# A weight remainder accumulated from DRAM, and the small start loads on two other queues, in a two-layer flow backbone

## The chip, the cores and the metric

One core of one Trainium2 chip. The metric is the device time of one execution in microseconds (us). The kernel before takes 2303.33 us, the median of three runs (2302.43, 2303.33 and 2305.74 us).

## What is computed

Two layers of a backbone on 128 context tokens and 512 latent tokens, 1024 channels, all in float32. Each layer modulates the normalised tokens, sends them through one wide input projection (11264 columns), runs four branches on its pieces (convolution, Hyena with an FFT, pooling, attention), gates and merges them, and projects the result back:

```python
def parallel_mixer(h, p, latent, k_ctx, v_ctx):
    u = h @ p['w_in']                                   # 1024 x 11264
    (a_glu, a_gate, b_proj, b_gate, c_in, c_gate, q, k, v, d_gate, g_merge) = jnp.split(u, points, axis=-1)
    ya = conformer_conv(a_glu, ...)                     # GLU, depthwise conv 31, layer norm, swish, pointwise
    ya = (ya * jax.nn.silu(a_gate)) @ p['wo_conv']
    filt = hyena_filters(L, ...)                        # a small MLP on positions gives the filters
    yb = (hyena(b_proj, ..., filt, ...) * jax.nn.silu(b_gate)) @ p['wo_hyena']
    yc = (multiscale_pool(c_in, p['pool_w'], ...) * jax.nn.silu(c_gate)) @ p['wo_pool']
    att = block_attention(rope(rms_norm(q)), rope(rms_norm(k)), v)
    yd = (att * jax.nn.silu(d_gate)) @ p['wo_attn']
    gm = jax.nn.sigmoid(g_merge).reshape(B, L, 4, D_MODEL)
    return (gm[:, :, 0] * ya + gm[:, :, 1] * yb + gm[:, :, 2] * yc + gm[:, :, 3] * yd) @ p['w_out'], k, v

def trunk_layer(x, cond, p, ...):
    shift, scale, gate = jnp.split(jax.nn.silu(cond) @ p['w_ada'] + p['b_ada'], 3, axis=-1)
    h = rms_norm(x, p['norm_g']) * (1.0 + scale) + shift
    y, k, v = parallel_mixer(h, p, ...)
    return x + gate * y, k, v
```

## The kernel before, in words

**Products.** TensorE multiplies in a float32 form of reduced precision. To keep float32 accuracy every factor is split in two, `hi` (the value rounded to that form) and `lo` (what is left), and each product is three matmuls: hi x hi, hi x lo, lo x hi. For a weight these are the tiles `whi` and `wlo`.

**The ring of weights.** `weights` (L331) brings in one weight tile of 128 partitions and at most 1024 columns: eight blocks of 128 rows by 128 columns for `w_in` and `wo_attn`, four blocks of 128x128 for `wo_hyena` and `wo_pool`, four blocks of 128x256 for queries, keys, values and `w_out`, one of 128x128 for `pool_w`. SyncE loads it to `raw` (two buffers, NRAW), ScalarE casts it to `whi` (three buffers, NHI), and `wlo` (three buffers) is made in one of two ways. While `pooled[0]` is set (from the first Hyena inputs on, and off again for the gates of the convolution and for the output projection), ScalarE writes -whi into `wlo` and a DMA that GpSimd issues adds `raw` to it, in SBUF (L344 and L345). Otherwise VectorE subtracts (L347). The ring holds three tiles: the next load is issued when a raw buffer is free, and a raw buffer is free when all that read it have ended, the cast and the accumulating DMA among them.

```python
            sp.dma_start(out=rv.rearrange("p (k c) -> p k c", k=kk), in_=src)
            act.copy(hi[:, 0:w], rv)
            if pooled[0]:
                act.activation(out=lo[:, 0:w], in_=r32(hi[:, 0:w]), func=AF.Copy, scale=-1.0)
                nc.gpsimd.dma_start(out=r32(lo[:, 0:w]), in_=rv, accum_op=ALU.add)
```

178 tiles take the first way. The weights are loaded in the order in which TensorE uses them; in the code such tiles have a priority ahead of the work around them (WAHEAD).

**Who sets the order.** `Loom` (L85) is a planner that runs while the program is written: work is cut into threads, and it lets the thread write its next piece whose operands are ready first by its own model of TensorE, of the element engines and of the DMA. TensorE's order is exactly the one so written; the other engines' is set by a scheduler of its own. So a load's arrival time, as `load` (L324) models it, can move matmuls, and tile numbers such as raw_121 differ between two programs without meaning anything.

**The start.** The loads of the start are written by hand, in the order of the string DORD (L32): `0` to `7` are chunks of the conditioning weight `w_ada` (two loads each, `load_chunk`, L1935; the first chunks borrow the tiles of the weight ring, raw, wlo and whi), `f`, `g`, `h`, `i` what the Hyena filters read (`fetch`, L856: decay, hy_w3, hy_b3), `x` the tokens (`load_x`, L676), `t` the FFT tables, and `s` the small loads: seven for the hidden layers of the filters (`load_hidden`, L549: zfeat, w1, b1, freq, b2 and two blocks of w2), `sel`, ten rows of parameters (`load_params`, L516) and `edge`. `load_small` (L1929) writes a few of them after each larger load (SMALL is 3 per half chunk). All of them are issued by SyncE. Ahead of them come `c_ctx`, `c` and the identity. The thread `cond` (L531) turns the conditioning rows with ScalarE's tanh, and the products with `w_ada` wait for it.

**The layer.** The first 72 us hold the start: filters, modulation, the first products with `w_ada`. Then come, for each layer, the Hyena inputs with the filters beside them, queries, keys and values, attention beside the FFT convolution, the merges of the four branches with the convolution and the pooling between them, and the output projection. GpSimd sums squares of the filters, works in the pooling, and issues the accumulating DMAs.

Of the kernel before, what the change touches and what calls it, by code (L numbers as in the profile page):

```python
# [10 lines left out]
F32R = mybir.dt.float32r  # L11
I32 = mybir.dt.int32
AF = mybir.ActivationFunctionType
ALU = mybir.AluOpType
# [14 lines left out]
NSLOT = 13  # L29
NRAW = 2  # L30
NHI = 3
DORD = "0sf4xt15gh2637"  # L32
SMALL = 3
PT = 6.5
PN = 4.0
HW = 80
# [30 lines left out]
def r32(ap):  # L67
    return ap.bitcast(F32)
# [165 lines left out]
def hybrid_flow_backbone(ctx: ExitStack, tc: tile.TileContext, i, o):  # L234
    nc = tc.nc
    lm = Loom()
# [4 lines left out]
    sp = nc.sync  # L241
# [18 lines left out]
    def nm(p):  # L260
        count[0] += 1
        return f"{p}{count[0]}"
# [58 lines left out]
            dve.scalar_tensor_tensor(out=lo, in0=src, scalar=scale, in1=r32(hi),  # L321
                                     op0=ALU.mult, op1=ALU.subtract)

    def load(dst, src):  # L324

        sp.dma_start(out=dst, in_=src)  # L326
        lm.issue = max(lm.issue, lm.pe - 2.0) + 0.48
        lm.dma = max(lm.dma, lm.issue + 1.2) + int(np.prod(dst.shape)) * 4 / 360e3
        return lm.dma + 1.9

    def weights(src, kk, n):  # L331
        yield from wr.get()
        lm.bg = True
        with tc.high_priority(offset=WAHEAD):
            raw = wp.tile([P, 1024], F32, tag="raw", name=nm("raw"), bufs=NRAW)
            hi = wp.tile([P, 1024], F32R, tag="whi", name=nm("whi"), bufs=NHI)
            lo = wp.tile([P, 1024], F32R, tag="wlo", name=nm("wlo"), bufs=NHI)
            w = kk * n
            rv = raw[:, 0:w]
            sp.dma_start(out=rv.rearrange("p (k c) -> p k c", k=kk), in_=src)  # L340
            act.copy(hi[:, 0:w], rv)
            if pooled[0]:

                act.activation(out=lo[:, 0:w], in_=r32(hi[:, 0:w]), func=AF.Copy, scale=-1.0)  # L344
                nc.gpsimd.dma_start(out=r32(lo[:, 0:w]), in_=rv, accum_op=ALU.add)  # L345
            else:
                dve.tensor_tensor(out=lo[:, 0:w], in0=rv, in1=r32(hi[:, 0:w]), op=ALU.subtract)  # L347
        lm.bg = False
        return (hi[:, 0:w].rearrange("p (k c) -> p k c", k=kk),
                lo[:, 0:w].rearrange("p (k c) -> p k c", k=kk))  # L350

    def w_cols(l, c0):
        return weights(i["w_in"][l][:, c0:c0 + 128].rearrange("(k p) c -> p k c", p=P), 8, 128)
# [58 lines left out]
    def token_proj(src, a, fn):  # L412


        bank = {}
        for kh in range(2):
            whi, wlo = yield from weights(src[512 * kh:512 * kh + 512].rearrange("(k p) c -> p k c", p=P), 4, 256)
            for t in (1, 2, 3, 4, 0):
                b = (t + 1) // 2
                first = kh == 0 and t in (0, 1, 3)  # L420
                if first:
                    bank[b] = yield from mm.get()
                else:
                    yield
                out = bank[b][:, 0:256] if t in (0, 1, 3) else bank[b][:, 256:512]
                cols = slice(128 * t, 128 * t + 128)
                for k in range(4):
                    ah, al = a.h(4 * kh + k)[:, cols], a.l(4 * kh + k)[:, cols]
                    last = kh == 1 and k == 3
                    for n, (x, y) in enumerate(((ah, whi), (al, whi), (ah, wlo))):  # L430
                        pe.matmul(out, x, y[:, k, :], start=(first and k == 0 and n == 0),
                                  stop=(last and n == 2), skip_group_check=True)
                if t == 0:
                    wr.put(WD)
                if kh == 1 and t in (0, 2, 4):
                    if t:
                        yield from fn(t - 2, bank[b].rearrange("p (t c) -> p t c", t=2))
                    else:
                        yield from fn(-1, bank[b][:, 0:256].unsqueeze(1))
                    mm.put()  # L440
# [75 lines left out]
    def load_params(s):  # L516
        rows = s.v(0, 512)
        b = 0
        r = []
        for src in (i["conv_dw_w"].rearrange("l k c -> (l k) c"), i["conv_dw_b"], i["conv_ln_g"], i["conv_ln_b"],  # L520
                    i["hy_short_w"].rearrange("l k (j c) -> (l k j) c", j=3),
                    i["hy_short_b"].rearrange("l (j c) -> (l j) c", j=3),
                    i["hy_skip"].rearrange("l k c -> (l k) c"), i["pool_scale"],
                    i["norm_g"].rearrange("l (j c) -> (l j) c", j=2),
                    i["b_ada"].rearrange("l (j c) -> l j c", c=512)[:, 0:4]):
            n = int(np.prod(src.shape[:-1]))
            r.append((rows[b:b + n, :], src, t_prm))
            b += n
        return r
# [19 lines left out]
    def load_hidden(s):  # L549

        w1, w2, cols = s.v(T, P), s.v(T + P, P), s.v(T + 2 * P, 3)
        r = [(s.v(0, T)[0:33, :], i["c_zfeat"]),
             (w1[0:33, :].rearrange("z (l h) -> z l h", l=2), i["hy_w1"].rearrange("l z h -> z l h"))]
        for c, n in enumerate(("hy_b1", "hy_freq", "hy_b2")):
            r.append((cols[:, c:c + 1], i[n].rearrange("l (h a) -> (l h) a", a=1)))
        dve.memset(w2, 0.0)
        for l in range(DEPTH):
            h = slice(64 * l, 64 * l + 64)
            r.append((w2[h, h], i["hy_w2"][l]))
        return [x + (t_hid,) for x in r]  # L560
# [35 lines left out]
    def w_ada(l, j):  # L596
        return i["w_ada"][l][:, 256 * j:256 * j + 256].rearrange("(k p) c -> p k c", p=P)
# [78 lines left out]
    def load_x(xs, prompt, sample):  # L676
        for h in range(2):
            v = xs[h].v(0, 5, 512)
            load(v[:, 0, :], prompt[:, 512 * h:512 * h + 512])
            t = load(v[:, 1:5, :], sample[:, 512 * h:512 * h + 512].rearrange("(j p) d -> p j d", p=P))  # L680
        return t
# [153 lines left out]
    class Hyena:  # L835
# [12 lines left out]
        def tables(self, s):  # L848
            self.tabE = s
            t = load(s.v(0, 2560), i["c_tab"])  # L850
            self.tf = s.v(0, 4, 2, 128)
            self.ti = s.v(1024, 4, 2, 128)
            self.tpr = s.v(2048, 4, 128)
            self.ev_tab.t = t
# [1068 lines left out]
    small = load_hidden(s_hid) + [(sel, i["c_sel"], t_prm)] + load_params(s_prm) + [(edge, i["c_edge"], t_prm)]  # L1923
# [2 lines left out]
    h0 = hys[0]  # L1926
    xs0 = [Slot(), Slot()]

    def load_small(n):  # L1929

        for dst, src, t in small[:n]:
            t[0] = load(dst, src)
        del small[:n]

    def load_chunk(j):  # L1935

        if spare:
            s, halves = None, []
            for _ in range(2):
                tag = spare.pop()  # L1940
                t = wp.tile([P, 1024], F32, tag=tag, name=nm(tag), bufs=NRAW if tag == "raw" else NHI)
                halves.append(t.rearrange("p (k c) -> p k c", k=4))
        else:
            s = Slot()
            v = s.v(0, 8, 256)
            halves = [v[:, 0:4], v[:, 4:8]]
        for kh in range(2):
            t = load(halves[kh], w_ada(0, j)[:, 4 * kh:4 * kh + 4])
            load_small(SMALL)
        chunks.append((j, s, halves, t))  # L1950

    for x in DORD:
        if x == "x":
            x_first = (xs0, sm.tile([P, 5, 2], F32, tag="ssq0", name=nm("ssq")),
                       load_x(xs0, i["x_prompt"][0], i["x_sample"][0]))
            load_small(2 * SMALL)
        elif x in "fghi":
            c, q = divmod("fghi".index(x), 2)
            if c not in h0.flt:
                h0.flt[c] = Slot()  # L1960
            h0.fetch(c, q)
        elif x == "t":
            h0.tables(Slot())
            load_small(2 * SMALL)
        elif x == "s":
            load_small(7)
        else:
            load_chunk(int(x))
    load_small(len(small))
    t_hid, t_prm = t_hid[0], t_prm[0]  # L1970
    lm.spawn(cond(s_cond, t_cond), 0)
    lm.spawn(hidden(s_hid, t_hid), 1)
# [102 lines left out]
```

## Time and profile before

| | |
|---|---|
| median of three runs | 2303.33 us |
| the profiled execution, its own time | 2302.68 us |
| its span | 2300.9 us |
| TensorE, matmuls (PE) | 2201.6 us busy, 96% |
| TensorE, weight loads (PEld, beside PE) | 2154.2 us, 94% |
| VectorE (DVE) | 1416.2 us, 62% |
| ScalarE (ACT) | 1104.7 us, 48% |
| GpSimd (POOL) | 348.8 us, 15% |

Times on the page are microseconds of one profiled execution. Issuing a DMA is not counted as busy. PEclk is the clock that was granted to TensorE, in tenths of full speed (2.4 GHz; the lower level is 1.2 GHz). The span cut into 40 slices has 57.5 us in each. The page's DMA rows tell two queues apart: q1 holds the loads and stores that SyncE issues, q0 those that GpSimd issues. A row `A <- B` of the waits says that engine A stood idle until B had ended.

### The profile page before, as it was taken

How to read it: one execution, taken by the hardware profiler on the slowest of the kernel's cores; microseconds unless marked ns; L12 is line 12 of the kernel's file. 1: busy time of each engine (PE TensorE's matmuls, PEld its weight loads, DVE VectorE, ACT ScalarE, POOL GpSimd, SP SyncE). 2: the span in 40 equal slices, each digit the busy share in tenths (PEclk: the TensorE clock that was granted, in tenths of full speed). 3: DMA queues.
4: the chain of work that ended last, by engine and by line, in shares of the span. 5: the costliest groups of instructions: out<-in, count | busy, mean ns of one | idle time of the engine just before them, and what ended most of it. 6: DMA issues, size and time to landing. Idle time of an engine off the chain costs nothing.

```text
span 2300.9 us, 39784 instructions
## 1 busy us (share of the span) xinstructions
PE 2201.6 (96%) x15951; PEld 2154.2 (94%) x15951; DVE 1416.2 (62%) x2853; ACT 1104.7 (48%) x2078; POOL 348.8 (15%) x348
## 2 busy tenths in 40 slices
PE   5998999999999999999989999999999999999999
PEld 3998999999999998999979999999999999899999
DVE  5785786556669854334466668756656897533433
ACT  4644456666664334223355453667667433422321
POOL 1633211000001111000045242000000111100000
PEclk8999999999999999999999999999999999999999
DMA  8465564444446655233545434444344576432332
GB/s 273 117 153 135 132 167 105 104 101 99 116 115 150 150 123 120 76 95 87 168 129 120 115 87 118 105 109 102 81 102 100 141 151 153 105 100 78 97 105 79
DMA packets 310440, 274.08 MB, mean 119 GB/s; under 512 B 11293, under 2 KB 279773, under 8 KB 309998
## 3 DMA queue, kind: packets, MB, share of 16 engines
q1 hardware_dynamic: 284622, 186.59, 26.9%
q0 software_dynamic: 25632, 84.95, 20.2%
q8 instruction: 125, 2.05, 0.4%
q14 instruction: 61, 0.50, 0.1%
HBM read 174.34 MB, written 12.22 MB: 81 GB/s over the span
## 4 chain that ended last, share of the span: by engine, by line
PE 75%; DVE 12%; DMA 5%; ACT 3%; issue 3%; POOL 1%; SPq 1%; POOLq 0%; ACTq 0%; DVEq 0%
PE mm L194 60%; DVE sl L179 6%; PE ax L194 6%; PE sc L194 5%; PE ax L203 4%; DVE wx L179 2%; DMA wlo<-raw 2%; DMA raw<-in_w_in_dram 1%; DVE k L179 1%; ACT u L179 1%; POOL sl L179 1%; SPq L326 1%; DVE u L179 1%; ACT wlo L179 1%; DMA sl<-in_hy_w_dram 1%
## 5 line engine op out<-in xcount | busy, mean ns | idle before, releaser
L194 PE MATMUL mm<-sl,whi 128*128 128x320 f32 x6304 | 1427.2, 314 | 7.7 <-DVE t L179 5.5
L194 PEld LDWEIGHTS mm<-sl,whi 128*128 128x128 f32 x6304 | 1058.1, 190 | 15.1 <-DVE t L179 4.8
L194 PE MATMUL mm<-sl,wlo 128*128 128x320 f32 x3152 | 982.8, 312 | 6.8 <-DMA wlo<-raw 5.9
L194 PEld LDWEIGHTS mm<-sl,wlo 128*128 128x128 f32 x3152 | 597.5, 190 | 7.6 <-DMA wlo<-raw 6.4
L179 ACT CAST whi<-raw 128x1024 fp32r<-128x1024 f32 (+2 forms) x272 | 255.4, 939 | 581.8 <-PE mm L194 419.8
L345 POOL DMA_DIRECT2D wlo<-raw x178 | 154.6, 868 | 1140.9 <-ACT wlo L179 844.3
L194 PE MATMUL mm<-whi,sl 128*128 128x256 f32 x1600 | 289.8, 283 | 0.0
L194 PEld LDWEIGHTS mm<-whi,sl 128*128 128x128 f32 x1600 | 244.9, 188 | 1.6 <-issue 0.8
L179 DVE TENSOR_TENSOR wlo<-raw,whi 128x1024 fp32r<-128x1024 f32 x94 | 95.6, 1017 | 225.1 <-ACT whi L179 224.8
L194 PE MATMUL mm<-wlo,sl 128*128 128x256 f32 x800 | 224.1, 280 | 0.8 <-DMA wlo<-raw 0.8
L194 PE MATMUL sc<-sl,sl 128*128 128x128 f32 (+1 forms) x1344 | 208.4, 298 | 10.2 <-DVE sl L179 3.9
L179 DVE SCALAR_TENSOR_TENSOR sc<-sl,prm,sc 128x640 f32<-128x640 f32 (+14 forms) x232 | 207.2, 893 | 11.2 <-ACT sc L179 6.7
L179 DVE TENSOR_TENSOR h<-ax,h 128x512 fp32r<-128x512 f32 (+1 forms) x200 | 120.6, 604 | 131.3 <-ACT h L179 130.2
L194 PEld LDWEIGHTS sc<-sl,sl 128*128 128x128 f32 x1344 | 182.4, 197 | 13.6 <-DVE u L179 5.2
L179 ACT ACTIVATE wlo<-whi 128x1024 fp32r<-128x1024 f32 (+2 forms) x178 | 174.6, 981 | 1.6
L179 DVE SCALAR_TENSOR_TENSOR t<-t,mm 128x320 f32<-128x320 f32 x192 | 93.1, 485 | 133.2 <-PE mm L194 101.5
L179 ACT ACTIVATE t<-mm 128x320 f32<-128x320 f32 x208 | 89.9, 432 | 130.8 <-PE mm L194 130.5
L194 PEld LDWEIGHTS mm<-wlo,sl 128*128 128x128 f32 x800 | 150.8, 189 | 1.0 <-DMA wlo<-raw 1.0
L179 ACT CAST h<-ax 128x512 fp32r<-128x512 f32 (+1 forms) x200 | 102.5, 514 | 70.4 <-PE ax L203 68.3
L179 DVE TENSOR_SCALAR_CACHE_REDUCE u<-sc,rq 128x640 f32<-128x640 f32 x128 | 112.7, 880 | 38.0 <-PE sc L194 36.7
L194 PE MATMUL ax<-h,sl 128*128 128x256 f32 (+1 forms) x656 | 121.8, 298 | 4.8 <-DVE h L179 4.5
L179 ACT ACTIVATE u<-u,nb 128x640 f32<-128x640 f32 x128 | 106.2, 829 | 37.8 <-DVE u L179 37.0
(194 smaller groups left out, 2208.8 us busy)
## 6 DMA issues: line engine op xcount, KB each, us to landing
raw<-in_w_in_dram SPq DMA_DIRECT2D x176, 512.0 KB
wlo<-raw POOLq DMA_DIRECT2D x152, 512.0 KB, 4.7
wlo<-in_w_ada_dram SPq DMA_DIRECT2D x19, 512.0 KB
whi<-in_w_ada_dram SPq DMA_DIRECT2D x19, 512.0 KB
raw<-in_wo_attn_dram SPq DMA_DIRECT2D x16, 512.0 KB
raw<-in_w_out_dram SPq DMA_DIRECT2D x16, 512.0 KB
sl<-in_c_decay_dram SPq DMA_DIRECT2D x16, 320.0 KB
mscr<-t SPq DMA_DIRECT2D x16, 320.0 KB
```

The source lines that it names most:

```text
L179: r = f(*args, **kw)
L194: r = self.real.matmul(out, lhsT, rhs, **kw)
L203: r = self.real.transpose(out, in_, ident)
L326: sp.dma_start(out=dst, in_=src)
L345: nc.gpsimd.dma_start(out=r32(lo[:, 0:w]), in_=rv, accum_op=ALU.add)
```

## The change

Two edits. The accumulating DMA reads the weight from its place in DRAM again and no more from `raw`; it has the shape of the raw load, so a tile of eight blocks is 1024 runs of 512 bytes, and so is its target written. `raw` is then read by the cast (or by VectorE's subtraction) alone. And the nineteen small loads of the start are written ahead of everything in DORD: the first seven are issued by ScalarE, the other twelve by GpSimd, with an arrival in the planner of 12 us or later. SyncE issues the larger loads, in the same order as before.

```diff
-DORD = "0sf4xt15gh2637"
-SMALL = 3
+DORD = "0f4xt15gh2637"
...
-    def load(dst, src):
-        sp.dma_start(out=dst, in_=src)
+    def load(dst, src, eng=None):
+        (eng or sp).dma_start(out=dst, in_=src)
+        if eng:
+            lm.dma = max(lm.dma, lm.pe + 1.2) + int(np.prod(dst.shape)) * 4 / 360e3
+            return max(lm.dma + 1.9, 12.0)
         lm.issue = max(lm.issue, lm.pe - 2.0) + 0.48
...
                 act.activation(out=lo[:, 0:w], in_=r32(hi[:, 0:w]), func=AF.Copy, scale=-1.0)
-                nc.gpsimd.dma_start(out=r32(lo[:, 0:w]), in_=rv, accum_op=ALU.add)
+                nc.gpsimd.dma_start(out=lo[:, 0:w].rearrange("p (k c) -> p k c", k=kk), in_=src.bitcast(F32R),
+                                    accum_op=ALU.add)
...
-    def load_small(n):
-        for dst, src, t in small[:n]:
-            t[0] = load(dst, src)
-        del small[:n]
+    for n, (dst, src, t) in enumerate(small):
+        t[0] = load(dst, src, nc.scalar if n < 7 else nc.gpsimd)
...
             t = load(halves[kh], w_ada(0, j)[:, 4 * kh:4 * kh + 4])
-            load_small(SMALL)
```

The other calls of `load_small` go too. What moves on the engines, at three places:

SyncE's queue at the start, before, from its fourth load on (sl_116 is what the hidden layers read, sl_117 the parameters, sl_138 the filters' decay and weights):

```order
L326 DMA raw_121<-in_w_ada_dram 128x4x256
L326 DMA sl_116<-in_c_zfeat_dram 33x640
L326 DMA sl_116<-in_hy_w_dram 33x2x64
L326 DMA sl_116<-in_hy_b_dram 128x1
L326 DMA raw_122<-in_w_ada_dram 128x4x256
L326 DMA sl_116<-in_hy_freq_dram 128x1
L326 DMA sl_116<-in_hy_b_dram 128x1
L326 DMA sl_116<-in_hy_w_dram 64x64 x2
L326 DMA sel<-in_c_sel_dram 128x2
L326 DMA sl_117<-in_conv_dw_w_dram 62x512
L326 DMA sl_117<-in_conv_dw_b_dram 2x512
L326 DMA sl_117<-in_conv_ln_g_dram 2x512
```

The same place in the change (sl_144 holds the decay now, sl_119 and sl_120 the tokens x):

```order
L325 DMA raw_140<-in_w_ada_dram 128x4x256
L325 DMA raw_141<-in_w_ada_dram 128x4x256
L325 DMA sl_144<-in_c_decay_dram 128x5x128
L325 DMA sl_144<-in_hy_w_dram 64x2x128
L325 DMA sl_144<-in_hy_b_dram 2x2x128
L325 DMA wlo_148<-in_w_ada_dram 128x4x256
L325 DMA whi_149<-in_w_ada_dram 128x4x256
L325 DMA sl_119<-in_x_prompt_dram 128x512
L325 DMA sl_119<-in_x_sample_dram 128x4x512
L325 DMA sl_120<-in_x_prompt_dram 128x512
L325 DMA sl_120<-in_x_sample_dram 128x4x512
```

The fourth half chunk of `w_ada` and the first load of x come right behind the filters' loads; the nineteen small ones are gone from this queue.

ScalarE at the start, in the change (hd is a scratch tile, sl_112 holds the conditioning rows; before, the table load stood first):

```order
L325 DMA sl_116<-in_c_zfeat_dram 33x640
L325 DMA sl_116<-in_hy_w_dram 33x2x64
L325 DMA sl_116<-in_hy_b_dram 128x1
L325 DMA sl_116<-in_hy_freq_dram 128x1
L325 DMA sl_116<-in_hy_b_dram 128x1
L325 DMA sl_116<-in_hy_w_dram 64x64 x2
L178 ACT_TABLE_LOAD
L178 ACTIVATE hd_190<-ones 2x640
L178 ACTIVATE sl_112<-sl_112 2x1024
```

Seven loads (the last row is two) stand ahead of the table load and of the tanh on the conditioning rows.

GpSimd among the filter sums of the first layer, before (k, sl and wx are tiles of the filters, frs a scale, fv sums):

```order
L345 DMA wlo_1223<-raw_1221 128x1024
L179 TENSOR_TENSOR frs_1154<-fv_1153,nhalf 128x2
L179 TENSOR_TENSOR sl_538<-sl_450,sl_138 128x640
L345 DMA wlo_1329<-raw_1327 128x1024
L179 TENSOR_TENSOR wx_189<-sl_450 128x128 x2
L179 TENSOR_TENSOR k_1165<-k_1165,k_1179 128x512
```

The same place in the change:

```order
L347 DMA wlo_1315<-in_w_in_dram 128x8x128
L178 TENSOR_TENSOR frs_1213<-fv_1212,nhalf 128x2
L178 TENSOR_TENSOR sl_508<-sl_437,sl_144 128x640
L178 TENSOR_TENSOR wx_189<-sl_437 128x128 x2
L347 DMA wlo_1423<-in_w_in_dram 128x8x128
L178 TENSOR_TENSOR k_1236<-k_1236,k_1391 128x512
```

The accumulating DMAs stand at much the same places among the sums; each now reads eight runs for each of 128 partitions where it read one.

## Rows read from the trace of the kernel before

**Rows 1.** the page: busy times, and the span in 40 slices
```profile
PE 2201.6 (96%) x15951; PEld 2154.2 (94%) x15951; DVE 1416.2 (62%) x2853; ACT 1104.7 (48%) x2078; POOL 348.8 (15%) x348
...
PEclk8999999999999999999999999999999999999999
```

**Rows 2.** windows: us, busy PE, PEld, DVE, ACT, POOL, clock, DMA, GB/s
```profile
0.00:50.00 50.00, 25.24 (x158) 11.98 (x162) 24.17 (x73) 20.63 (x47) 6.12 (x10) 0.80 0.84 269
850.00:900.00 50.00, 42.39 (x257) 41.09 (x256) 30.73 (x65) 23.52 (x41) 6.96 (x8) 0.90 0.50 113
```

**Rows 3.** waits of PE from 72 us on: total us, times, longest
```profile
PE ax L203 <- DVE sl L179: 15.2, 6, 5.8
PE mm L194 <- DMA wlo<-raw: 6.7, 3, 3.3
PE mm L194 <- DVE t L179: 5.5, 6, 2.6
```

**Rows 4.** waits of SP's queue, the whole span
```profile
SPq L340 <- DMA wlo<-raw: 1351.8, 176, 21.5
...
SPq L326 <- DMA sl<-in_conv_dw_w_dram: 1.6, 1, 1.6
```

**Rows 5.** timeline of SP, 0 to 60 us: start us, us, what
```profile
1.84 0.43 SPq L326 DMA_DIRECT2D raw<-in_w_ada_dram  x1
...
5.16 1.45 SPq L326 DMA_DIRECT2D sl<-in_hy_w_dram  x2
...
18.08 0.43 SPq L326 DMA_DIRECT2D sl<-in_x_sample_dram  x1
```

**Rows 6.** windows of the start, columns as in rows 2
```profile
5.00:20.00 15.00, 6.43 (x33) 3.36 (x34) 5.76 (x8) 2.57 (x4) 0.00 (x0) 1.00 0.65 180
20.00:40.00 20.00, 9.50 (x60) 3.62 (x60) 12.20 (x40) 10.71 (x30) 0.00 (x0) 0.67 0.99 341
40.00:50.00 10.00, 9.30 (x68) 5.00 (x71) 5.47 (x19) 3.55 (x10) 5.92 (x6) 0.64 1.04 334
```

**Rows 7.** chain of waits, 0 to 75 us: start us, us, what
```profile
44.02 8.58 DMA sl<-in_w_ada_dram
```

**Rows 8.** the tile wlo, whole span: ns min/median/max, first and last start
```profile
L345 POOL DMA_DIRECT2D wlo<-raw x178: 850/869/1024, 93.0 to 2019.6; - x178
```

**Rows 9.** timeline of ACT, POOL and PE around 740 us
```profile
730.54 1.05 ACT L179 CAST whi<-raw 128x1024 fp32r<-128x1024 f32 x1 [2.90 <-PE mm L194]
...
737.61 1.05 ACT L179 CAST whi<-raw 128x1024 fp32r<-128x1024 f32 x1 [2.90 <-PE mm L194]
...
740.23 0.87 POOL L345 DMA_DIRECT2D wlo<-raw  x1 [6.20 <-ACT wlo L179]
...
744.62 0.46 PE L194 MATMUL mm<-sl,whi 128*128 128x320 f32 x2
```

**Rows 10.** DMA issues, whole span: KB each, median us to landing
```profile
wlo<-raw POOLq DMA_DIRECT2D x152, 512.0 KB, 4.7
```

**Rows 11.** timeline of ACT, POOL and PE around 890 us
```profile
887.96 1.05 ACT L179 CAST whi<-raw 128x1024 fp32r<-128x1024 f32 x1 [2.34 <-DMA raw<-in_w_in_dram]
...
890.89 0.87 POOL L345 DMA_DIRECT2D wlo<-raw  x1 [6.86 <-ACT wlo L179]
...
896.87 0.48 PE L194 MATMUL mm<-sl,wlo 128*128 128x320 f32 x1 [2.58 <-DMA wlo<-raw]
```

**Rows 12.** DMA queues from 750 to 800 us: packets, MB, share
```profile
q0 software_dynamic: 1052, 3.85, 40.7%
q1 hardware_dynamic: 7280, 3.67, 24.9%
```

**Rows 13.** DMA queues from 872.9 to 876.4 us, with one accumulation of 64 KB
```profile
q0 software_dynamic: 144, 0.07, 15.5%
```

**Rows 14.** windows from 75 to 125 us, columns as in rows 2
```profile
75.00:100.00 25.00, 25.00 (x193) 24.23 (x192) 17.65 (x45) 14.40 (x31) 18.02 (x17) 1.00 0.37 99
```

**Rows 15.** DMA issues, 1860 to 1960 us, columns as in rows 10
```profile
wlo<-raw POOLq DMA_DIRECT2D x15, 512.0 KB, 5.5
```

More of the change, by code (lines that the diff above doesn't have):

```diff
@@ L1955, in hybrid_flow_backbone @@
                        load_x(xs0, i["x_prompt"][0], i["x_sample"][0]))
-            load_small(2 * SMALL)
         elif x in "fghi":
@@ L1963, in hybrid_flow_backbone @@
             h0.tables(Slot())
-            load_small(2 * SMALL)
-        elif x == "s":
-            load_small(7)
         else:
             load_chunk(int(x))
-    load_small(len(small))
     t_hid, t_prm = t_hid[0], t_prm[0]
```

## Prediction

> **What bounds the kernel now.** I read the page first: TensorE is busy 2201.6 of 2300.9 us, at a clock that is full in all but a few slices [rows 1]. The two parts of the change touch none of its matmuls, only their order, so all that can be won or lost is its idle time (99 us in all) and the half-clock stretches behind some of it. I then read the waits: what does TensorE wait for, and where? Some 25 us of the idle time lies in the first 50 us, while the first loads come in (PE busy 25.24 of 50 us); single stretches later lose up to 8 us, the one from 850 us 7.6 with the clock down to 0.90 [rows 2]. After 72 us the waits that end on a wlo tile come to 6.7 us, in three places; most others end on VectorE, in the filters and the convolutions [rows 3]. Against that, SyncE sits 1351.8 us before the next raw load until a wlo DMA has landed [rows 4]. That is no loss by itself, since the ring has three whi/wlo tiles; the reader should see that the long wait is SyncE's and the short one TensorE's.
>
> **Part 1, the start.** SyncE issues in order, and 19 of its first 33 DMAs are small. They take it about as long as the large ones, 0.4 us each, or more (1.45 us for the two of hy_w); it reaches the last load of x only at 18.08 us [rows 5]. Meanwhile the DMA engines are not full: a share of 0.65 from 5 to 20 us, then 0.99 and more [rows 6]. The idle part is 15 x 0.35 = 5.2 us. From 20 us on the transfers are the bound until the last w_ada chunk lands at 52.6 us, for which TensorE waits [rows 7]. The bytes stay the same, so the end of the transfers can come forward by what was idle: at most 5.2 us. Two things take some of it back. ScalarE now issues seven loads first, at 0.4 us each by SyncE's rows some 3 us, and the order shows its table load and the conditioning tanh behind them; the first w_ada product waits for that tanh, but the last chunk, which sets the end, doesn't. And SyncE's loads wait for older ones that used the same semaphore (1.6 us on conv_dw_w once [rows 4]), so it can now trip over ScalarE's loads in the first microseconds, where its raw w_ada load stood at 1.84 us before [rows 5]. I take 4 us of 5.2, with 0 and 8 as ends: 8 if x, which SyncE reaches 11 us of issuing earlier, helps the VectorE chain behind it as well. GpSimd's twelve loads are covered: its queue is empty until after 40 us (0 busy from 5 to 40 us, 5.92 us from 40 to 50) [rows 6], and twelve issues of 0.87 us [rows 8] are done by 13 us. Without that cover each would delay the first filters by 0.87 us.
>
> **Part 2, what it removes.** The accumulating DMA no longer reads raw, so a raw tile is free when its cast to whi ends, not when the wlo DMA lands. In the regular stretches that is about 7 us earlier: cast from 737.61, negation, DMA issued at 740.23 [rows 9], landing 4.7 us after the issue by the median [rows 10]. Where it costs now: at 887.96 ScalarE's cast had waited 2.34 us for raw, the wlo DMA went out at 890.89 and TensorE stood 2.58 us until 896.87 [rows 11]; the 3.3 us wait of rows 3 is the same place in the second layer. I count 5 of the 6.7 us as gone, and 1 us of clock behind them.
>
> **What it adds.** All 178 DMAs now read rows of the weight in DRAM. A projection tile of 128x1024 is then 1024 runs of 512 bytes instead of 128 of 4 KB (the raw load of the same bytes shows it: 7280 packets for seven tiles, 1040 each with 16 for the semaphore); tiles of 4x256 are runs of 1 KB. Three prices.
> (a) The packets. Accumulating 4 KB takes 0.407 x 16 x 50 us / 940 = 346 ns [rows 12]. The 64 KB tiles of pool_w are already 512-byte runs: 0.155 x 16 x 3.5 us / 128 = 68 ns [rows 13], so 4 KB would be 542 ns. A tile goes from 2.8 to 4.3 us of all 16 engines, +1.6 us. Those reads are from SBUF; from DRAM it is not shown. Plain loads in the same window take 0.249 x 16 x 50 us / 7280 = 27 ns a packet, so the source as such is not slow.
> (b) The issue. GpSimd takes 850 to 1024 ns, whatever the bytes, but always for 128 runs [rows 8]. For 1024 runs nothing here shows it. Ends: nothing more, or eight times, 6.95 us. I take 1.7 us, +0.8: nearest is the row on its own engine, in which 64 KB and 512 KB cost the same, so a fixed part dominates; an estimate. Behind it on GpSimd stand the filter sums; it is 72% busy from 75 to 100 us [rows 14], where five such DMAs cost perhaps 1 us of TensorE.
> (c) Collisions get rarer: raw loads start at a landing now, so they run into the next accumulation (5.5 us to land in the densest stretch against the median of 4.7 [rows 10, 15]). Starting at the cast they are 2.5 us ahead of it. I take -0.7 us.
> So a tile lands some 1.7 us later. What covers that is the time between landing and first use. In the regular stretch a tile of TensorE work is 7.07 us (cast to cast, 730.54 to 737.61) and the next two tiles are in hand: the one cast at 730.54 is used at 744.62 and landed at 740.23 - 7.07 + 4.7 = 737.9, so 7 us are in hand [rows 9]. I made the same reading for all 178, from the first, issued at 93.0, to the last, at 2019.6 [rows 8]: the median is 7.4 us, but 12 have under 1.7, 20 under 3, 29 under 4, 58 under 6. The shortfalls add up to 12 us at 1.7 later, 34 at 3, 57 at 4, 145 at 6, 214 at 7. About half of the 12 were late through their raw, which goes: I count 6. If a stall goes, next late is VectorE's t [rows 3].
>
> The Trainium skill speaks on (b): its page "DMA: Bandwidth & Descriptors", section "Anatomy of one DMA — SWDGE (gpsimd) path", calls descriptor generation small and says many descriptors can be emitted before they cost. By it (b) would be nothing and the sum some 3 us lower; no row here has more than 128 runs to agree or not.
>
> **Sum.** Start -4, waits for wlo -5, clock -1, later landings +6, filters +1, and -3 for what stands behind SyncE's shorter wait, stores and filter loads (an estimate with ends of -8 and +5, since the planner also writes another order on TensorE): -6 us. The profiled execution took 2302.68 us, 0.65 below the median of 2303.33, so I forecast 2297.5.
>
> **Rivals.**
> *The issue grows with the runs* (slower). GpSimd spends 3 to 7 us on each of the 152 large tiles. It decides from about 2.7 us, where the shortfalls reach what was won. At 4 us landings are 4 later: 2303 - 12 + 29 to 57, some 2330; at 6.95, 7 later, up to 214 of shortfall and the filter chain with it, 2420 to 2500. For it: the time is GpSimd's own, and it has eight times as many runs to name. Against: no dependence on anything in rows 8, with ends 0.17 us apart.
> *The DMA engines become the bound* (slower). In the dense stretch 40.7% becomes 64%, with 24.9% of loads 89% [rows 12]: still cover. If a packet from DRAM took 90 ns, 5.8 + 1.8 us would pass the 7.07 us of a tile: 0.5 us on each of some 35 tiles a layer, about +30, 2320. The same page, section "Why small descriptors are slow (HBM only)", says small runs cost on the DRAM side and not between SBUF tiles; rows 12 and 13 contradict the second half (68 ns against 346/8 = 43), so I don't lean on the first.
> *Nothing arrives* (no change). The start is hidden, because VectorE's and ScalarE's chain from 52.6 to 72 us isn't shortened, and the later landings eat what the raw tiles give: 2303, within 4 us.
>
> **How the numbers follow.** Forecast 0.47, issue 0.20, engines 0.10, nothing 0.23. About 0.2% (4.6 us) is what a measurement can tell: faster is under 2298.7, slower over 2307.9. Faster 0.45 (0.42 of the forecast's share, 0.03 of nothing's), same 0.24 (0.05 and 0.19), slower 0.31 (0.20, 0.10, 0.01). Alone, the forecast reaches from 2284 to 2303. The range is 2282 to 2330: below by start -8 and a lucky order, above to the issue at 4 us; beyond it I leave the issue's upper half (0.10) and 0.06 below.
>
> **What would show it.** Right: the last w_ada transfer lands near 48 us; DMA shares from 5 to 20 us over 0.8; GpSimd's DMA under 2.5 us, landing in 5.5 to 7; SyncE's wait on wlo gone, in its place one on the cast; PE's waits for wlo under 10 us; the engines' share from 750 to 800 us near 0.9. Wrong: an issue of over 2.7 us, or PE idle that ends on wlo between 100 and 340 us, where the least is in hand.

## The result and the profile after

The changed kernel takes 2319.59 us, the median of four runs (2317.34 to 2321.08), beside 2303.64 us for the kernel before on the same chip: a ratio of 1.0067, 95% interval 1.005 to 1.0085. It is slower by 0.7%, where I forecast 0.25% faster. The time lies in the upper part of the range, on the side to which I gave 0.31.

The page of the changed kernel, busy times and DMA queues (packets, MB, share of 16 engines), from the execution of 2321.08 us:

```profile
PE 2207.9 (95%) x15951; PEld 2157.2 (93%) x15951; DVE 1425.5 (61%) x2853; ACT 1102.8 (48%) x2078; POOL 465.1 (20%) x360
...
PEclk7999999999999999999989999999999999999999
...
q0 software_dynamic: 156864, 85.21, 29.1%
q1 hardware_dynamic: 283476, 186.19, 26.8%
```

The accumulation queue on the page of the kernel before:

```profile
q0 software_dynamic: 25632, 84.95, 20.2%
```

TensorE is busy 6.3 us longer than in [rows 1], and idle for 111.4 us instead of 99.3. The mean granted clock is 0.976 here and 0.980 before, but over the four executions it runs from 0.976 to 0.983, and the two at 0.983 still took 2317 and 2320 us; so the loss is not one of the clock. GpSimd's 465.1 us (348.8 before) include the issues of its DMAs: on this engine they do count as busy, unlike what I wrote beside the table of the kernel before. The accumulation queue has 156864 packets instead of 25632 for the same bytes, and the loads' queue hardly changed (284622 before). Windows, columns as in rows 2:

```profile
0.00:50.00 50.00, 30.04 (x200) 15.69 (x201) 25.61 (x81) 23.18 (x50) 6.66 (x16) 0.80 1.00 310
850.00:900.00 50.00, 47.66 (x318) 46.00 (x317) 33.03 (x67) 27.18 (x49) 11.46 (x9) 1.00 0.66 124
5.00:20.00 15.00, 8.48 (x50) 4.30 (x50) 6.22 (x11) 6.60 (x11) 2.73 (x6) 1.00 1.05 329
20.00:40.00 20.00, 11.55 (x63) 4.80 (x64) 13.54 (x44) 11.49 (x32) 0.00 (x0) 0.60 1.08 347
750.00:800.00 50.00, 50.00 (x342) 50.00 (x341) 46.27 (x63) 18.78 (x24) 12.49 (x8) 1.00 0.87 150
```

Beside [rows 2, 6]: the engines are full from 5 us on (1.05 instead of 0.65), and TensorE is busy 30.04 of the first 50 us instead of 25.24. From 850 to 900 us it is busy 47.66 us instead of 42.39 at the full clock; the change is some 12 us later there, and by the ends of the weight tiles it won 6.3 us between 860 and 905 us of before. So something is won in the places named; how much of it comes from the DRAM source is asked below. The loss must be elsewhere. Waits of PE from 72 us on (total us, times, longest):

```profile
PE mm L193 <- DMA wlo<-in_w_in_dram: 32.7, 14, 7.6
PE sc L193 <- DVE sl L178: 6.0, 4, 2.0
```

Waits of SyncE's queue, the whole span, the two largest:

```profile
SPq L342 <- ACT whi L178: 635.7, 79, 22.1
SPq L342 <- ACT t L178: 432.0, 51, 20.9
```

SyncE waits for the cast now, as foreseen, and no more for a wlo DMA [rows 4]. But TensorE's waits for wlo went from 6.7 us in three places [rows 3] to 32.7 us in fourteen. Not all of these 26 us are lost: its waits that end on VectorE fell from some 49 to some 32 us. The tile wlo, whole span (ns min/median/max, first and last start):

```profile
L347 POOL DMA_DIRECT2D wlo<-in_w_in_dram x136: 1274/1552/1747, 93.0 to 2041.0; - x136
...
L347 POOL DMA_DIRECT2D wlo<-in_pool_w_dram x8: 891/897/907, 860.4 to 2029.3; - x8
```

DMA issues of the whole span (KB, median us to landing):

```profile
wlo<-in_w_in_dram POOLq DMA_DIRECT2D x136, 512.0 KB, 6.5
```

The issue is 1.55 us for 1024 runs and still 0.90 for the 128 of pool_w [rows 8]; the median landing went from 4.7 to 6.5 us [rows 10]. Between 72 and 345 us, while layer 0's filters run, it is worse. DMA issues of that stretch, in the kernel before:

```profile
wlo<-raw POOLq DMA_DIRECT2D x22, 512.0 KB, 4.9
```

And in the change:

```profile
wlo<-in_w_in_dram POOLq DMA_DIRECT2D x22, 512.0 KB, 8.0
```

The longest landing of that stretch, 11.7 us, belongs to the tile that GpSimd issued at 216.44 us. SyncE's timeline there:

```profile
216.02 0.37 SPq L619 DMA_DIRECT2D whi<-in_w_ada_dram  x1
216.56 0.83 SPq L619 DMA_DIRECT2D wlo<-in_w_ada_dram  x1
```

Two halves of a w_ada chunk, 512 KB each, went out beside it; until 228.1 us the engines were full. The tile issued just before it, at 213.66 us, landed at 221.6, and TensorE stood for it:

```profile
221.66 0.63 PE L193 MATMUL mm<-sl,wlo 128*128 128x320 f32 x1 [5.24 <-DMA wlo<-in_w_in_dram]
```

I read the ends of all 272 weight tiles in both traces. The change is 2.6 us ahead after the seventh tile (153 us of before), 11 us behind at 352 us, 7 behind at 1010 us, 12 at 1440 and 18 at 2050.

### The profile page after: what moved, and what is told of

The parts are those of the page before. It is cut to its first block, busy times and chain, and to the rows that moved or that the text cites. A ratio compares the mean times of both kernels' runs of the same rounds, so it can differ in the third digit from the quotient of the medians.

```text
span 2319.3 us, 39693 instructions
## 1 busy us (share of the span) xinstructions
PE 2207.9 (95%) x15951; PEld 2157.2 (93%) x15951; DVE 1425.5 (61%) x2853; ACT 1102.8 (48%) x2078; POOL 465.1 (20%) x360
## 3 DMA queue, kind: packets, MB, share of 16 engines
q0 software_dynamic: 156864, 85.21, 29.1%
## 4 chain that ended last, share of the span: by engine, by line
PE 79%; DMA 7%; DVE 5%; issue 4%; ACT 2%; POOL 1%; SPq 1%; ACTq 0%; POOLq 0%; DVEq 0%
PE mm L193 63%; PE sc L193 6%; PE ax L193 6%; DMA wlo<-in_w_in_dram 5%; PE ax L202 4%; DVE sl L178 3%; POOL sl L178 1%; DVE wx L178 1%; DMA sl<-in_hy_w_dram 1%; SPq L325 1%; DVE k L178 1%; DMA mscr<-t 1%; DVE u L178 1%; ACT u L178 0%; DMA whi<-in_w_ada_dram 0%
## 5 line engine op out<-in xcount | busy, mean ns | idle before, releaser
L347 POOL DMA_DIRECT2D wlo<-in_w_in_dram x136 | 206.0, 1517 | 786.3 <-ACT wlo L178 492.7
L193 PE MATMUL mm<-whi,sl 128*128 128x256 f32 x1600 | 295.1, 286 | 1.7 <-ACT t L178 1.5
L178 DVE TENSOR_TENSOR wlo<-raw,whi 128x1024 fp32r<-128x1024 f32 (+1 forms) x94 | 96.0, 1022 | 224.4 <-ACT whi L178 224.1
L193 PE MATMUL sc<-sl,sl 128*128 128x128 f32 (+1 forms) x1344 | 207.6, 298 | 13.3 <-DVE sl L178 6.0
L202 PE MATMUL ax<-ident,u 128*128 128x128 f32 x752 | 119.4, 274 | 4.3 <-DVE sl L178 1.7
```

What stands on the lines that cost most here:

```text
L178: r = f(*args, **kw)
L193: r = self.real.matmul(out, lhsT, rhs, **kw)
L202: r = self.real.transpose(out, in_, ident)
L347: nc.gpsimd.dma_start(out=lo[:, 0:w].rearrange("p (k c) -> p k c", k=kk), in_=src.bitcast(F32R), accum_op=ALU.add)
```

## The experiments

Two theories stood against each other. A: the accumulations land too late. B: the planner wrote another, worse order of TensorE, because `load` tells it other arrivals. (Where TensorE's order differs, the other engines' order can differ with it; "order" below means both, and no run tells them apart. In all the runs called old order the sequence of TensorE's matmuls in the trace is that of before.) The first four kernels separate the two parts, the order, and the source of the accumulation.

**The start alone.** The change with its own order of TensorE, the accumulation from raw:

```diff
-                nc.gpsimd.dma_start(out=lo[:, 0:w].rearrange("p (k c) -> p k c", k=kk), in_=src.bitcast(F32R),
-                                    accum_op=ALU.add)
+                nc.gpsimd.dma_start(out=r32(lo[:, 0:w]), in_=rv, accum_op=ALU.add)
```

> The small start loads on ScalarE and GpSimd, the accumulation from raw in SBUF as before; TensorE's order is that of the change. Theory A (the loss comes from the accumulations that land later: TensorE's waits for wlo went from 6.7 to 32.7 us): the start's gain of about 5 us is left, 2295 to 2300 us, and the waits for wlo are 10 us or less. Theory B (the planner's other order of TensorE, which the new arrival times bring, costs the time): 2312 to 2322 us, though the accumulation is the old one.

2306.11 us against 2304.76, ratio 1.0005 (0.9996 to 1.0013). Neither theory's range holds: nothing won and nothing lost. Its waits of PE for wlo from 72 us on are 12.8 us:

```profile
PE mm L193 <- DMA wlo<-raw: 12.8, 7, 4.0
```

**DRAM alone.** The kernel before with the change's accumulation; TensorE's order is exactly that of before.

```diff
-                nc.gpsimd.dma_start(out=r32(lo[:, 0:w]), in_=rv, accum_op=ALU.add)
+                nc.gpsimd.dma_start(out=lo[:, 0:w].rearrange("p (k c) -> p k c", k=kk), in_=src.bitcast(F32R),
+                                    accum_op=ALU.add)
```

> The accumulation reads DRAM, the start loads stay on SyncE as before; TensorE's order is that of before. Theory A: slower by what the change lost and the start gave back, 2316 to 2328 us, with waits for wlo of 25 us or more, most of them while the filters run. Theory B: 2296 to 2306 us, with waits for wlo under 12 us.

2308.29 us, ratio 1.001 (1.0001 to 1.002). Between the two theories: 3.5 us slower, with 14.0 us of waits for wlo:

```profile
PE mm L194 <- DMA wlo<-in_w_in_dram: 14.0, 7, 3.5
```

Each part alone costs 0.1% or nothing; together they cost 0.7%.

**The start, with the old order.** The small loads are issued by the other two engines, and the planner is told the old times (`load` without a source issues nothing and only counts the time):

```diff
-        sp.dma_start(out=dst, in_=src)
+        if src is not None:
+            sp.dma_start(out=dst, in_=src)
...
+    for n, (dst, src, t) in enumerate(small):
+        (nc.scalar if n < 7 else nc.gpsimd).dma_start(out=dst, in_=src)
     def load_small(n):
         for dst, src, t in small[:n]:
-            t[0] = load(dst, src)
+            t[0] = load(dst, None)
```

> The small loads are issued by ScalarE and GpSimd, but the planner is told the arrival times of before, so TensorE's order is that of before; the accumulation reads raw. If the start is worth its 5 us of DMA time by itself: 2297 to 2300 us, the same as with the change's order or a little better. Rival (the gain lies in the order that the new arrivals bring, or the time until 75 us is set by other work): 2302 to 2305 us.

2303.75 us, ratio 0.9995 (0.9986 to 1.0003): nothing, as the rival had it. Its windows, columns as in rows 2:

```profile
5.00:20.00 15.00, 6.43 (x32) 3.15 (x32) 5.98 (x9) 5.47 (x8) 2.68 (x6) 1.00 1.06 334
...
40.00:50.00 10.00, 6.02 (x46) 3.44 (x45) 8.96 (x21) 3.20 (x8) 6.04 (x6) 0.78 1.11 335
```

Its waits of PE up to 72 us, the longest three:

```profile
PE ax L203 <- DVE sl L179: 8.7, 1, 8.7
PE sc L194 <- ACT sl L179: 5.7, 1, 5.7
PE ax L203 <- ACT k L179: 4.6, 3, 3.6
```

The engines are full from 5 us, but VectorE and ScalarE become the wait: VectorE is busy 8.96 of the 10 us from 40 to 50 (5.47 before [rows 6]). The first weight tile is cast at 57.9 us, before at 57.7.

**Short runs from SBUF.** A gap of one element between the blocks of raw makes the accumulation 1024 runs of 512 bytes as well, with raw held until it lands (l3 is wlo as blocks; to make room, two constants share a tile):

```diff
-            raw = wp.tile([P, 1024], F32, tag="raw", name=nm("raw"), bufs=NRAW)
+            raw = wp.tile([P, 1032], F32, tag="raw", name=nm("raw"), bufs=NRAW)
...
-            rv = raw[:, 0:w]
+            rv = raw[:, 0:kk * (n + 1)].rearrange("p (k c) -> p k c", k=kk)[:, :, 0:n]
...
-                nc.gpsimd.dma_start(out=r32(lo[:, 0:w]), in_=rv, accum_op=ALU.add)
+                nc.gpsimd.dma_start(out=r32(l3), in_=rv, accum_op=ALU.add)
...
```

> All as before, but the raw tile has a gap of 4 bytes between its blocks, so that the accumulation from SBUF is 1024 runs of 512 bytes too; raw stays held until it lands, and nothing reads DRAM a second time. Theory C (the later landing is the price of short runs: GpSimd names them for 1.55 us instead of 0.87, the engines take 68 ns for each): the median landing is 6.2 to 6.6 us as in the change, the time 2312 to 2330 us. Theory D (it is the DRAM side, or the raw load that now runs beside the accumulation): the issue is 1.55 us, but the landing 5.2 to 5.6 us, and the time 2305 to 2312 us.

2357.47 us, ratio 1.0238 (1.021 to 1.0266): theory C for the landing (6.7 us, just over its range), and a time beyond both. DMA issues of the whole span here:

```profile
wlo<-raw POOLq DMA_DIRECT2D x152, 512.0 KB, 6.7
```

The accumulation queue from 750 to 800 us here:

```profile
q0 software_dynamic: 7280, 3.67, 60.7%
```

The same row of the change:

```profile
q0 software_dynamic: 7566, 3.82, 61.7%
```

The tile wlo here, GpSimd's issues:

```profile
L346 POOL DMA_DIRECT2D wlo<-raw x178: 887/1546/1995, 94.2 to 2075.4; - x178
```

ScalarE's waits for raw here:

```profile
ACT whi L179 <- DMA raw<-in_w_in_dram: 108.7, 25, 8.5
ACT whi L179 <- DMA raw<-in_wo_attn_dram: 105.0, 15, 10.8
```

The same in the kernel before:

```profile
ACT whi L179 <- DMA raw<-in_wo_attn_dram: 40.1, 8, 6.4
ACT whi L179 <- DMA raw<-in_w_in_dram: 37.8, 10, 6.2
```

A packet of 512 bytes (of each tile's 1040, 1024 carry data) takes 0.607 x 16 x 50 us / 7168 = 68 ns from SBUF, and 0.617 x 16 x 50 / 7450 = 66 ns from DRAM. The issue is 1.55 us in both. So the price is that of the runs, whatever they are read from, and what DRAM brings is the early release of raw: with the same runs the change's source is worth 2357 - 2308 = 49 us. In the change ScalarE waits for a raw load in one place only (5.9 us), in the kernel before for 87 us in all, here for over 200 us. (The rule of the Trainium skill that transfers inside SBUF don't suffer from small descriptors, "DMA: Bandwidth & Descriptors", section "Why small descriptors are slow (HBM only)", is not borne out for accumulating DMAs: inside SBUF 512 bytes cost 68 ns as a run of their own and 346 / 8 = 43 ns within a run of 4 KB [rows 12].)

That left the surplus of 13 us to explain. **Both parts with the old order** (the diff of the start with the old order and the DRAM source together), and **the change with a third order** (one constant of the planner):

```diff
-            return max(lm.dma + 1.9, 12.0)
+            return max(lm.dma + 1.9, 16.0)
```

> Both parts of the change, with TensorE's order of before (the planner is told the old arrival times). Alone, neither part cost more than 0.1%, and together they cost 0.7%. Theory E (what the two do to each other goes through the order of TensorE that the new arrivals bring): the sum of the parts, 2304 to 2310 us. Theory F (it goes through the hardware: the queues or the earlier start itself): 2314 to 2322 us, as the change.

> The change with one constant moved: the planner takes the small loads to arrive at 16 us at the earliest instead of 12, which gives a third order of TensorE; DMAs are those of the change. Theory E, with the order as luck: another time than the change's, by 5 us or more, most likely in 2304 to 2316 us. Theory F, or an order that is worse for a reason of its own: within 3 us of the change's 2319.6.

2305.97 us, ratio 1.0 (0.9989 to 1.0011), and 2309.0 us, ratio 1.0023 (1.0012 to 1.0034): theory E twice. The very same DMAs take 2306, 2309 or 2320 us, by TensorE's order. (Single executions of the first of these spread from 2296 to 2307 us, and its profiled one, 2294.2 us of span, lies at the fast end; positions read from one execution are good to some us.)

**Where DRAM wins and where it loses.** In the old order, the first 19 accumulations from raw and the others from DRAM, and the reverse:

```diff
+                if late[0]:
+                    nc.gpsimd.dma_start(out=lo[:, 0:w].rearrange("p (k c) -> p k c", k=kk), in_=src.bitcast(F32R),
+                                        accum_op=ALU.add)
+                else:
+                    nc.gpsimd.dma_start(out=r32(lo[:, 0:w]), in_=rv, accum_op=ALU.add)
...
+    late = [False]
...
             at.gD = yield from slots(2)
+            late[0] = True
```

The reverse asks `not late[0]`.

> The start and TensorE's order of before; the first 19 accumulations, up to the end of the queries of layer 0 (about 340 us), read raw, the other 159 read DRAM. With reading DRAM alone, 11 us were lost up to 352 us and 5 to 6 won after it. If the two stretches are independent: 2298 to 2301 us, faster than both. Rival (what the late part won was only the stall that the early part had moved): 2303 to 2307 us.

> The other half: the first 19 accumulations read DRAM, the other 159 raw. If the stretches are independent: the 8 to 11 us lost by 340 us stay, 2312 to 2317 us. Rival (the later stages take the delay up): 2304 to 2309 us.

2300.93 us, ratio 0.9985 (0.9977 to 0.9994), and 2310.71 us, ratio 1.0022 (1.0012 to 1.0032), against 2304.31. So early costs 6.4 us (less than the 8 to 11 expected), late wins 3.4, and their sum, +3.0, is close to the 3.5 us of DRAM alone: the stretches are independent as far as these differences tell, each good to some 2 us.

**The same rule in the change's order**, and a later turn in both orders (45 accumulations from raw, up to the end of layer 0's first merge):

```diff
             yield from merge(l, 1, hy.gb, 4, i["wo_hyena"][l], None, "first")
             hy.gb.free()
+            late[0] = True
```

> The change with its own order of TensorE, but the first 19 accumulations (up to about 340 us) read raw, the other 159 DRAM. Theory G (the new order loses in the later stages too, where three tiles in a row fall due together: TensorE stood 7.6 us at 1664 us and 2.8 at 1570): some 5 us over the kernel with the start loads alone, 2309 to 2313 us. Theory H (what the new order loses with DRAM is all in the filters of layer 0): 2301 to 2306 us.

> The start and TensorE's order of before; the first 45 accumulations, up to the end of layer 0's first merge (about 600 us), read raw, the other 133 DRAM. By the ends of the tiles of the late version (6 us lost by 594 us, 9 won after it): 2295 to 2299 us, faster than every version so far. Rival (the 4 us between 350 and 594 us were one execution's chance): 2300 to 2302 us, as the late version.

> The same rule in the change's order of TensorE: 45 accumulations from raw, 133 from DRAM. Theory G: the later stages still lose, 2308 to 2314 us. Theory H: 2299 to 2305 us.

Against 2305.68 us: 2313.77 for the first rule in the new order (ratio 1.0039, 1.0025 to 1.0053), **2293.65 for the later turn in the old order (0.9953, 0.9937 to 0.9969)** and 2314.0 for the later turn in the new one (1.0036, 1.0022 to 1.005); the first a little over its range, the second a little under. Theory G holds: the new order loses behind the filters as well, and the same rule that makes the old order 12 us faster than before leaves the new one 8 us slower. The middle one beats both kernels. Its waits of PE from 72 us on:

```profile
PE mm L194 <- DMA wlo<-in_w_in_dram: 5.4, 2, 2.7
```

What it won can be seen around 880 us, in windows with the same matmuls, columns as in rows 2; first before, then here:

```profile
843.00:916.00 73.00, 65.39 (x408) 63.74 (x407) 37.95 (x75) 32.77 (x59) 8.70 (x10) 0.93 0.49 115
845.60:912.30 66.70, 61.17 (x408) 59.42 (x408) 37.76 (x75) 32.74 (x59) 12.76 (x10) 1.00 0.67 122
```

Timeline of PE there, before:

```profile
883.98 0.90 PE L194 MATMUL mm<-sl,whi 128*128 128x320 f32 x2 [2.58 <-DVE t L179]
```

And in the kernel with the later turn:

```profile
883.05 0.54 PE L194 MATMUL mm<-sl,whi 128*128 128x320 f32 x2 [0.30 <-DVE t L179]
894.74 0.39 PE L194 MATMUL mm<-sl,wlo 128*128 128x320 f32 x1 [2.66 <-DMA wlo<-in_w_in_dram]
```

The wait that went is one for VectorE's t (2.58 to 0.30 us); the wait for wlo behind it stayed (2.58 us in [rows 11], 2.66 here). Idle time fell by 2.1 us and, at a clock of 1.00 instead of 0.93, the same matmuls took 4.2 us less. Over the whole span 7.7 of the 10.9 us between the two profiled executions are busy time of TensorE; since the clock differs from one execution to the next, how much of that the source brings is open.

The new order can be followed matmul by matmul, as the start alone has the very same one. Beside it the change is 11.5 us behind at 352 us, 8.1 from 905 to 1300 us, and 17.9 at 1650 us; its largest steps back are at waits for wlo. One place shows such a step. Timeline of POOL (start us, us, idle before) in the kernel with the start alone, which accumulates from raw:

```profile
1641.86 0.86 POOL L347 DMA_DIRECT2D wlo<-raw  x1 [11.81 <-ACT wlo L178]
1644.53 0.86 POOL L347 DMA_DIRECT2D wlo<-raw  x1 [1.81 <-ACT wlo L178]
```

Timeline of PE there:

```profile
1646.45 0.58 PE L193 MATMUL mm<-wlo,sl 128*128 128x256 f32 x1 [3.96 <-DMA wlo<-raw]
```

The same place in the change, POOL:

```profile
1656.12 1.29 POOL L347 DMA_DIRECT2D wlo<-in_w_in_dram  x1 [10.89 <-ACT wlo L178]
1658.91 1.56 POOL L347 DMA_DIRECT2D wlo<-in_w_in_dram  x1 [1.49 <-ACT wlo L178]
```

And PE:

```profile
1664.42 0.55 PE L193 MATMUL mm<-wlo,sl 128*128 128x256 f32 x1 [7.64 <-DMA wlo<-in_w_in_dram]
```

Two whi buffers come free 3 us apart, so two accumulations go out 2.7 us apart, for a projection that TensorE has already begun. From raw the first landed 4.6 us after its issue and TensorE stood 4.0 us; in the change it landed after 8.2 us, with the second one and raw loads beside it (a share of 0.95 from 1656 to 1668 us), and TensorE stood 7.6. The wait is there again in the other two kernels with this order and late DRAM (7.5 and 6.9 us), while in the kernels with the old order no wait for wlo is over 3.7 us.

## Why the prediction was wrong, point by point

- **The start, -4.** Wrong: -1.0 us with the old order, an interval that holds zero. The transfers did end earlier (a share of 0.18 from 50 to 55 us with the old order, 1.15 before), but I took the last load to set the end although I had named VectorE's and ScalarE's chain behind it in "Nothing arrives", with 0.23. That rival was right for this part.
- **The issue, +0.8.** Right: 0.87 to 1.55 us, +0.7. (The Trainium skill's "DMA: Bandwidth & Descriptors", section "Anatomy of one DMA — SWDGE (gpsimd) path", calls descriptor generation small and has many descriptors go out before their cost shows; here 896 runs more do show, as 0.68 us, so it holds in part.) The slower rival built on eight times as much was wrong, and its 2330 us was near the time for another reason.
- **The packets, +1.6.** Right in size: 66 ns where I took 68. The share from 750 to 800 us is 0.87, as expected near 0.9, and TensorE is busy there for all 50 us. The rival with full engines in the dense stretch was wrong; that its 2320 us is the measured time is luck.
- **Collisions, -0.7.** Wrong in sign where it matters. From 700 to 1000 us a large tile lands 6.4 us after its issue by the median, +1.7. But in the filters' stage, where w_ada and filter loads run beside it, landings are 3.1 later, and in all 36 of the 178 take over 7.5 us, where 3 did before.
- **Later landings, +6.** This is the step that failed. I laid one shift of 1.7 us on all 178 tiles, with the time in hand as the trace of the old order had it. First, the tiles with the least time in hand (the filters' stage, as I had written) are the ones with the longest landings: that stretch alone costs 6.4 us in the old order and 2319.6 - 2313.8 = 5.8 in the new, as much as I had given to all. Second, in the new order the later stages cost 2313.8 - 2306.1 = 7.7 us more, where in the old order they win 3.4. In waits of TensorE for wlo, +6 and -5 made +1 us; measured are +26.0, with 13.3 us of such waits in five places between 100 and 340 us, the sign that I had given for wrong.
- **Waits for wlo, -5, and clock, -1.** The place was right, the wait was not. The wlo waits that I counted as gone still stand, 2.0 us at 904 and 2.6 at 2041 us in the change; what went around 880 us is a wait for VectorE's t, from 2.58 to 0.83 us, with the clock behind it. And of the 6.3 us given back between 860 and 905 us the start alone, which reads raw, gives back 4.5, so at most some 2 of them are the DRAM source's in this order. In the old order the late stretch as a whole is worth 3.4 us net of its own later landings, and 12 us if the first merge is left to raw as well.
- **The other order of TensorE, in "-3, with ends of -8 and +5".** The size failed: with the same DMAs it costs 2319.6 - 2306.0 = 13.6 us (the kernel before took 2303.6 and 2304.3 beside them). Between the start alone and the change, both in that order, waits for wlo rose by 19.9 us and the span by 16.4; in the old order by 7.3 and 5.7. Little of this is the order by itself: with raw it costs 2306.1 - 2303.8 = 2.4 us. Most is what it makes of DRAM behind the filters, 7.7 lost against 3.4 won. I read the time in hand from the old order's trace alone, and the new order had not yet been run. But the count would not have told: from landing to first use, counted alike, 10 of the 178 tiles have under 1.7 us in the old order and 11 in the new one with raw. I had no rival in which a new order and later landings act together.

What stays open: why the new order stands the later landings so much worse is shown at single places (1646 to 1664 us) and not as a general cause. Of the 12 us that the old order won with the later turn, the ends of the tiles put 6.3 between 843 and 916 us, 1.9 around 1340 and 4.3 from 1571 to 1681; but the last stretch gives back 3 us as well in the start with the old order and in DRAM early, which read raw there, so it is in part the profiled execution of before that was late. Whether a third raw buffer would bring the early release without the short runs was not tried; it takes 4 KB of each partition, and for the 64 bytes of the gaps two constants had already to share a tile.

## What to carry to other kernels

When a transfer gets longer, don't shift all its landings by the median: here the tiles with the least time in hand were those that share the engines with most other traffic. Change the source of a transfer only where its buffer is what is waited for, and keep the cheap form elsewhere. Of the 87 us for which ScalarE waits for raw in the kernel before, 3 lie ahead of 600 us, and the split at that point turned +0.1% into -0.5%; in the new order it left +0.4%, so it holds for one order at a time. And where a planner writes the order, test a change with the old order as well, or its effect can't be told from that of another order.

## What the runs showed of the hardware

An accumulating DMA pays 66 to 68 ns for a run of 512 bytes from DRAM and from SBUF alike, against 346 ns for 4 KB [rows 12] and 27 ns for a plain load's 512 bytes. GpSimd's issue goes from 0.87 to 1.30 us for 512 runs and 1.55 for 1024 (the 256 KB tiles of wo_hyena, four blocks, have the middle one).
